# Operand sums of the Strassen pairs moved into a reordered output projection, with 2 plain pairs ahead instead of 3

## Chip, core, metric

The kernel runs on one core of one Trainium2 chip. The metric is device microseconds of one execution, median of three runs.

## What is computed

One residual block of a streaming encoder, on x of 512 tokens by 1024 channels in float32. The parts that matter here are its last lines; `merged` is the gated sum of two attention branches.

```python
x = x + merged @ w_out
h2 = rmsnorm(x, g_ffn)
ff = silu(h2 @ w_ffn_gate) * (h2 @ w_ffn_up)     # 1024 -> 2816
x = x + ff @ w_ffn_down                          # 2816 -> 1024
```

## The kernel before, in words

Channels lie on the 128 partitions, tokens on the free axis, so an activation is a list of tiles of 128 by 512. Each float32 operand is split into a high and a low fp32r part, and every product is three matmuls (`mm3`, L205 to L209: high by high, high by low, low by high). A weight block of 128 by 1024 is loaded into a ring of 5 raw buffers (`wraw`, N_RAW). ScalarE (ACT) casts the high part `wh`, VectorE (DVE) subtracts to get the low part `wl`, both in rings of 4 (`wspl`). `Stream` (L97 to L142) does this for a list of weights in order, four loads ahead. A raw buffer is free for its next load when the `wl` of its old content is done, and the load is issued by the SP queue, which also issues the loads and stores below.

The **output projection** (L905 to L922) has 8 blocks, one per 128 output channels. Block d is 24 matmuls of 512 columns into one of four PSUM banks (`full_ct(mg)`). A residual tile `xr` is loaded from `xT` (L907), DVE adds the PSUM bank to it (L909, "the residual add"), SP stores the sum to `x2_scratch` (L910), ACT and DVE split it, scaled by the norm's gain, into `h2h` and `h2l` (L914, L915), ACT squares it (L918), and POOL adds the squares up (L922). The loads, splits and adds are put in an order for each engine by a scheduler, from the program's order.

Then come 22 **pairs**: gate and up projection of 128 channels of ff each. `KINDS` (L32) says which are plain and which are Strassen. A plain pair is 48 matmuls of 512 columns. A Strassen pair (L798 to L894) is one step of Strassen's scheme on a 2 by 2 split of weights and tokens: 7 products of 12 matmuls of 256 columns. Its right operands are tiles of h2 and the sums `s13` and `s24` of tiles k and 4 + k, made by `operand_sums(k)` (L927 to L939) for k = 0 to 3. That function first scales the two `xr` tiles in place on ACT, after their store to `x2_scratch` has read them; then DVE takes sums, ACT casts high parts, and DVE subtracts low parts.

Before, pairs 0, 1 and 2 are plain and run in a loop of their own (L943 to L973) by the scheduler, with weights out of the `Stream`. In pair 0 one matmul, `pn` (L947), sums the squares over the partitions, and ACT and DVE make the norm factor `r2` from it. The four operand sums stand in pairs 1 and 2. From pair 3 on (L986 to L1015) PE, DVE and ACT keep the order in which the program is written, with loads (`load`, `load_t`) two and three pairs ahead. Pair 21 is plain. The down projection follows (L1019 to L1031).

Of the kernel before, what the change touches and what calls it, by code (L numbers as in the profile page):

```python
# [10 lines left out]
F32R = mybir.dt.float32r  # L11
AF = mybir.ActivationFunctionType
ALU = mybir.AluOpType
AX = mybir.AxisListType

P = 128
S = 512
D = 1024
KT = D // P
# [8 lines left out]
N_BLK, N_RAW, N_SPLIT = 66, 5, 4  # L28
DA_ROUNDS, DA_STAGGER, DA_LEAD = 31, 7, 6
SB_ROUNDS, SB_STAGGER = 36, 4  # L30
N_FIRST = 3
KINDS = "PPP" + "S" * 18 + "P"  # L32


def units(kind, a, b):
# [9 lines left out]
def block_kernel(  # L45
# [17 lines left out]
    nc = tc.nc  # L63
# [11 lines left out]
    def B(dt=F32, name="b"):  # L75
        uid[0] += 1
        return blk.tile([P, S], dt, tag="b", name=f"{name}{uid[0]}")

    def PS(name="ps"):
        uid[0] += 1  # L80
        if name in ("pt", "pc"):
            return psf.tile([P, S], F32, tag="pf", name=f"{name}{uid[0]}")
        return psp.tile([P, S], F32, tag="ps", name=f"{name}{uid[0]}")

    def f(ap):
        return ap.bitcast(F32)
# [10 lines left out]
    class Stream:  # L97
# [35 lines left out]
        def next(self):  # L133
            i = self.at
            self.at += 1
            if i >= self.own:
                for j in range(i, i + self.SPLIT):
                    self.split(j)
            for j in range(i, i + self.AHEAD + 1):
                if j not in self.hl:  # L140
                    self.load(j)
            return self.hl.pop(i)  # L142

    srcs = [w_tc[i, c] for i in range(2) for c in range(4)]
# [9 lines left out]
        else:  # L154
            srcs.append(w_br[i, 1])
    srcs += [w_br[d, 0] for d in range(8)]
    srcs += [w_out[d] for d in range(8)]
    for n in range(N_FIRST):
        srcs += [w_fg[n], w_fu[n]]
    wd = Stream(  # L160
# [6 lines left out]
    for kt in range(KT):  # L167
# [4 lines left out]
        sl = slice((kt % 2) * S, (kt % 2 + 1) * S)  # L172
        nc.sync.dma_start(out=ws.raw[kt // 2][0][:, sl], in_=srcs[kt // 2][:, sl])
    g_mix, g_ffn, b_gate, g_sub = colt[:, 0:8], colt[:, 8:16], colt[:, 16:32], colt[:, 32:33]
# [7 lines left out]
    epst = const.tile([P, 1], F32, name="epst")  # L182
# [3 lines left out]
    ones = const.tile([P, S], F32, name="ones")  # L186
# [18 lines left out]
    def mm3(ps, w, a, first, last):  # L205
        (wh, wl), (ah, al) = w, a
        nc.tensor.matmul(out=ps, lhsT=wh, rhs=ah, start=first, stop=False)  # L207
        nc.tensor.matmul(out=ps, lhsT=wh, rhs=al, start=False, stop=False)  # L208
        nc.tensor.matmul(out=ps, lhsT=wl, rhs=ah, start=False, stop=last)  # L209
# [31 lines left out]
    def proj_ct(ps, acts, first=True, last=True, stream=None):  # L241
        wh, wl = (stream or ws).next()
        n = len(acts)
        for kt in range(n):
            sl = slice(kt * P, (kt + 1) * P)
            mm3(ps, (wh[:, sl], wl[:, sl]), acts[kt], first and kt == 0, last and kt == n - 1)
            if kt % 4 == 3 or kt == n - 1:
                yield

    def drain(gen):  # L250
        for _ in gen:
            pass
# [6 lines left out]
    def full_ct(acts, **kw):  # L259
        ps = kw.pop("ps", None) or PS("pc")  # L260
        drain(proj_ct(ps, acts, **kw))
        return ps
# [3 lines left out]
    acc = B(name="acc")  # L266
    nc.scalar.activation(out=acc, in_=xts[0], func=AF.Square)
    for kt in range(1, KT):
        sq = B(name="xsq")
# [435 lines left out]
    mg = []  # L705
    for d in range(8):
        ps = full_ct(o_a)
        nc.vector.tensor_tensor(out=gA[d], in0=gA[d], in1=ps, op=ALU.mult)
        nc.vector.tensor_tensor(out=gA[d], in0=gA[d], in1=mB[d], op=ALU.add)
        h, l = B(F32R, "mh"), B(F32R, "ml")  # L710
# [7 lines left out]
    def tt(o, a, b, op=ALU.add):  # L718
        nc.vector.tensor_tensor(out=o, in0=a, in1=b, op=op)  # L719
# [22 lines left out]
    class Plain(Pair):  # L742
# [23 lines left out]
        def prep_c(self):  # L766
            pass

        def matmuls(self, ps, hl, kts):
            for kt in kts:  # L770
                sl = slice(kt * P, (kt + 1) * P)
                mm3(ps, (hl[0][:, sl], hl[1][:, sl]), h2[kt], kt == 0, kt == KT - 1)

        def steps(self):
            self.pg, self.pu = PS("pc"), PS("pq")
# [119 lines left out]

    pairs = [(Strassen if k == "S" else Plain)(n) for n, k in enumerate(KINDS)] + [None] * 4

    def call(n, what):
        if n < NF:
            getattr(pairs[n], what)()  # L900

    x2d = nc.dram_tensor("x2_scratch", (KT, P, S), F32, kind="Internal").ap()
    x2, h2 = [], []
    acc = None
    for d in range(8):  # L905
        xr = B(name="xr")
        nc.sync.dma_start(out=xr, in_=xT[:, d])  # L907
        ps = full_ct(mg)
        nc.vector.tensor_tensor(out=xr, in0=ps, in1=xr, op=ALU.add)  # L909
        nc.sync.dma_start(out=x2d[d], in_=xr)  # L910
        x2.append(xr)
        h, l = B(F32R, "h2h"), B(F32R, "h2l")
        gc = g_ffn[:, d : d + 1]
        nc.scalar.activation(out=h, in_=xr, func=AF.Copy, scale=gc)  # L914
        nc.vector.scalar_tensor_tensor(out=l, in0=xr, scalar=gc, in1=f(h), op0=ALU.mult, op1=ALU.subtract)  # L915
        h2.append((h, l))
        sq = B(name="x2s")
        nc.scalar.activation(out=sq, in_=xr, func=AF.Square)  # L918
        if acc is None:
            acc = sq  # L920
        else:
            nc.gpsimd.tensor_tensor(out=acc, in0=acc, in1=sq, op=ALU.add)  # L922

    s13 = [(B(F32R, "s13h"), B(F32R, "s13l")) for _ in range(KT // 2)]
    s24 = [(B(F32R, "s24h"), B(F32R, "s24l")) for _ in range(KT // 2)]

    def operand_sums(k):  # L927
        u, v = x2[k], x2[4 + k]
        for d, y in ((k, u), (4 + k, v)):
            nc.scalar.activation(out=y, in_=y, func=AF.Copy, scale=g_ffn[:, d : d + 1])  # L930
        sa, sb = B(name="sa"), B(name="sb")
        tt(sa[:, lo_t], v[:, hi_t], u[:, hi_t], ALU.subtract)
        tt(sa[:, hi_t], u[:, lo_t], u[:, hi_t], ALU.subtract)
        split(*s13[k], sa)
        for o, a, b in ((lo_t, sa[:, lo_t], u[:, lo_t]), (hi_t, v[:, lo_t], sb[:, lo_t])):
            nc.vector.scalar_tensor_tensor(
                out=sb[:, o], in0=a, scalar=-1.0, in1=b, op0=ALU.mult, op1=ALU.subtract
            )
        split(*s24[k], sb)  # L939

    r2 = B(name="r2")
    ff = []
    for n in range(N_FIRST):  # L943
        pg = full_ct(h2)
        if n == 0:
            pn = PS("pn2")
            nc.tensor.matmul(out=pn, lhsT=ones[:, 0:P], rhs=acc, start=True, stop=True)  # L947
            nc.scalar.activation(out=r2, in_=pn, func=AF.Sqrt, scale=1.0 / D, bias=epst)
            nc.vector.reciprocal(out=r2, in_=r2)
            call(N_FIRST, "load_t")  # L950
        if n == 1:
            call(N_FIRST, "load")
            call(N_FIRST + 1, "load_t")
            operand_sums(0)
        if n == 2:
            call(N_FIRST + 1, "load")
            call(N_FIRST, "cast_a")
            call(N_FIRST, "low_a")
            call(N_FIRST + 2, "load_t")
            operand_sums(2)  # L960
        t1 = B(name="t1")
        nc.vector.tensor_tensor(out=t1, in0=pg, in1=r2, op=ALU.mult)
        nc.scalar.activation(out=t1, in_=t1, func=AF.Silu)
        pu = full_ct(h2)
        if n == 1:
            operand_sums(1)
        if n == 2:
            operand_sums(3)
            for what in ("sums", "prep_b", "prep_c"):
                call(N_FIRST, what)  # L970
            call(N_FIRST + 1, "cast_a")
        nc.vector.tensor_tensor(out=t1, in0=pu, in1=t1, op=ALU.mult)
        ff.append(t1)  # L973

    fs = []

    def split_ff():
# [5 lines left out]
    ET = mybir.EngineType  # L983
    last = max(n for n in range(NF) if KINDS[n] == "S")
    prev = None
    with tc.manual_schedule(engines={ET.PE, ET.DVE, ET.Activation}):  # L986
        for n in range(N_FIRST, NF):
            call(n + 2, "load")
            call(n + 3, "load_t")
            if prev:  # L990
                prev.silu()
                prev.tail()
            steps = pairs[n].steps()
            next(steps)
            call(n + 1, "low_a")
            if prev:
                prev.mul()
            call(n + 1, "sums")
            next(steps)
            call(n + 1, "prep_b")  # L1000
            next(steps)
            call(n + 1, "prep_c")
            if n > last:
                for j in range(3):
                    wd.load((n - last - 1) * 2 + j)
                for _ in range(6):
                    split_ff()
            if n == NF - 1:
                wd.split(0)
            next(steps)  # L1010
            call(n + 2, "cast_a")
            prev = pairs[n]
        prev.silu()
        prev.tail()
        prev.mul()  # L1015
# [3 lines left out]
    for d in range(8):  # L1019
        xr = B(name="xo")  # L1020
        nc.sync.dma_start(out=xr, in_=x2d[d])
        ps = full_ct(fs[0:8], last=False, stream=wd)
# [3 lines left out]
        for i in range(parts):  # L1026
            sl = slice(i * S // parts, (i + 1) * S // parts)
# [66 lines left out]
```

## Time and profile before

| What | Value |
|---|---|
| median of 3 runs | 731.52 us (731.46 to 731.79) |
| profiled execution | 732.07 us, span of its instructions 730.4 us |
| PE (TensorE matmul) busy | 722.8 us, 99% |
| DVE busy | 522.1 us, 71% |
| ACT busy | 367.1 us, 50% |
| DMA | 91.69 MB, mean 126 GB/s |

The profiled execution is 0.55 us above the median, and 1.7 us of it lie around the span. Busy time of PE is modelled from overlapping matmuls, so a PE shown as busy can still be late; starts of matmuls tell more. PE, PEld, DVE, ACT and POOL are compute engines, SP is the queue that issues most transfers.

### The profile page before, as it was taken

Reading aid. Unit: us, or ns where it says so; the run is one execution under the profiler, and the core shown is the slowest. Engines: PE = TensorE matmul, PEld = TensorE weight load, DVE = VectorE, ACT = ScalarE, POOL = GpSimd, SP = SyncE. Lnnn points to the kernel's source line nnn. Section 1 sums busy time; section 2 is a strip of 40 time slices with the busy share of each in tenths; the row PEclk is TensorE's granted clock in tenths of the full one; section 3 lists DMA queues with packets and bytes.
Section 4 is the critical chain, followed back from the end, with each engine's and each line's share of the span. In section 5 each row is a group of like instructions: output and inputs, shape, how many; then the busy total and the mean of one; then the engine's idle time right before and its main releaser. Section 6 shows DMA issues by size and latency. Waiting matters only on the chain.

```text
span 730.4 us, 10841 instructions
## 1 busy us (share of the span) xinstructions
PE 722.8 (99%) x4054; PEld 629.5 (86%) x4054; DVE 522.1 (71%) x871; ACT 367.1 (50%) x594; POOL 91.8 (13%) x135
## 2 busy tenths in 40 slices
PE   9999999999999999999999999999999999999997
PEld 6888788888888878888887899999999998888886
DVE  5865888777578887988447899999999978323330
ACT  5732666878566665644555544445445456221210
POOL 0267000000033222300220011111110000000000
PEclk9999999999999999999999999999999999999999
DMA  8953131122222121245653187776676124444300
GB/s 307 314 148 111 58 116 58 63 83 73 72 87 88 46 70 31 71 138 164 217 174 129 62 212 200 181 187 169 178 199 174 52 60 152 155 131 118 114 29 30
DMA packets 40068, 91.69 MB, mean 126 GB/s; under 512 B 4432, under 2 KB 5072, under 8 KB 40016
## 3 DMA queue, kind: packets, MB, share of 16 engines
q1 hardware_dynamic: 34832, 81.41, 34.4%
q0 software_dynamic: 4896, 9.44, 7.6%
q8 instruction: 32, 0.52, 0.3%
q10 hardware_dynamic: 288, 0.15, 0.1%
q14 instruction: 20, 0.16, 0.1%
HBM read 84.69 MB, written 4.19 MB: 122 GB/s over the span
## 4 chain that ended last, share of the span: by engine, by line
PE 89%; DMA 4%; DVE 3%; issue 2%; ACT 1%; POOL 1%; SPq 0%; DVEq 0%; POOLq 0%; ACTq 0%
PE pc L207 19%; PE pc L208 19%; PE pc L209 19%; PE pt L223 9%; PE pq L208 4%; PE pq L207 4%; PE pq L209 4%; PE pk L223 3%; DMA xr<-xT_dram 3%; PE sc L412 1%; PE sc L413 1%; DVE wl L90 1%; DVE xr L909 1%; PE ta L418 1%; PE tb L418 1%
## 5 line engine op out<-in xcount | busy, mean ns | idle before, releaser
L90 DVE TENSOR_TENSOR wl<-raw,wh 128x1024 fp32r<-128x1024 f32 (+2 forms) x98 | 106.1, 1084 | 85.4 <-ACT wh L89 76.9
L89 ACT CAST wh<-raw 128x1024 fp32r<-128x1024 f32 (+2 forms) x98 | 90.8, 930 | 151.7 <-PE pc L208 98.2
L207 PE MATMUL pc<-hh,wh 128*128 128x512 f32 x192 | 76.2, 397 | 0.0
L209 PE MATMUL pc<-hh,wl 128*128 128x512 f32 x192 | 75.3, 392 | 0.0
L208 PE MATMUL pc<-hl,wh 128*128 128x512 f32 x192 | 75.0, 391 | 0.0
L207 PE MATMUL pc<-fh,wh 128*128 128x512 f32 x176 | 68.5, 389 | 0.0
L208 PE MATMUL pc<-fl,wh 128*128 128x512 f32 x176 | 68.5, 389 | 0.0
L209 PE MATMUL pc<-fh,wl 128*128 128x512 f32 x176 | 68.5, 389 | 0.0
L806 POOL DMA_DIRECT2D t<-w_fg_dram x18 | 21.7, 1208 | 184.4 <-DVE tb L719 63.3
L209 PEld LDWEIGHTS pc<-hh,wl 128*128 128x128 f32 x192 | 36.0, 188 | 7.7
L208 PEld LDWEIGHTS pc<-hl,wh 128*128 128x128 f32 x192 | 36.1, 188 | 6.6
L207 PEld LDWEIGHTS pc<-hh,wh 128*128 128x128 f32 x192 | 36.1, 188 | 6.6
L207 PE MATMUL pc<-s13h,wht 128*128 128x256 f32 x144 | 40.8, 283 | 0.0
L208 PE MATMUL pc<-s13l,wht 128*128 128x256 f32 x144 | 40.8, 283 | 0.0
L209 PE MATMUL pc<-s13h,wlt 128*128 128x256 f32 x144 | 40.8, 283 | 0.0
L207 PEld LDWEIGHTS pc<-fh,wh 128*128 128x128 f32 x176 | 33.0, 188 | 6.9
L209 PEld LDWEIGHTS pc<-fh,wl 128*128 128x128 f32 x176 | 33.0, 188 | 6.9
L208 PEld LDWEIGHTS pc<-fl,wh 128*128 128x128 f32 x176 | 33.0, 188 | 6.7
L548 POOL TENSOR_SCALAR_AFFINE_SELECT om<-om 128x128 f32<-128x128 f32 x32 | 12.7, 398 | 202.8 <-ACT om L545 196.8
L737 ACT CAST whx<-rx 128x1024 fp32r<-128x1024 f32 x18 | 19.0, 1054 | 28.2 <-PE pq L208 17.5
L737 ACT CAST whv<-tb 128x512 fp32r<-128x512 f32 x36 | 20.7, 619 | 23.0 <-issue 15.7
L223 PE MATMUL pt<-wh,hh 128*128 128x512 f32 x96 | 30.5, 403 | 0.1
(287 smaller groups left out, 2048.4 us busy)
## 6 DMA issues: line engine op xcount, KB each, us to landing
t<-w_fg_dram POOLq DMA_DIRECT2D x18, 512.0 KB, 8.0
raw<-w_gate_dram SPq DMA_DIRECT2D x16, 512.0 KB, 3.2
raw<-w_dn_dram SPq DMA_DIRECT2D x16, 512.0 KB, 3.6
raw<-w_tc_dram SPq DMA_DIRECT2D x12, 512.0 KB, 5.0
t<-w_fu_dram SPq DMA_DIRECT2D x18, 256.0 KB, 5.9
t<-w_fg_dram SPq DMA_DIRECT2D x18, 256.0 KB, 6.7
rx<-w_fu_dram SPq DMA_DIRECT2D x18, 256.0 KB, 3.5
rx<-w_fg_dram SPq DMA_DIRECT2D x18, 256.0 KB, 4.4
```

Source lines behind the costliest of these rows:

```text
L89: a = nc.scalar.copy(out=h, in_=src)
L90: b = nc.vector.tensor_tensor(out=l, in0=src, in1=f(h), op=ALU.subtract)
L207: nc.tensor.matmul(out=ps, lhsT=wh, rhs=ah, start=first, stop=False)
L208: nc.tensor.matmul(out=ps, lhsT=wh, rhs=al, start=False, stop=False)
L209: nc.tensor.matmul(out=ps, lhsT=wl, rhs=ah, start=False, stop=last)
L223: nc.tensor.matmul(out=pss[tb], lhsT=hx[:, tb * P : (tb + 1) * P], rhs=wx[:, wsl], start=(k == 0 and i == 0), stop=(k == KT - 1 and i == 2),)
L412: nc.tensor.matmul(out=ps[:, o : o + w], lhsT=q[:, tb * P : w], rhs=kh[:, :w], start=True, stop=False)
L413: nc.tensor.matmul(out=ps[:, o : o + w], lhsT=q[:, tb * P : w], rhs=kl[:, :w], start=False, stop=True)
L418: nc.tensor.transpose(out=ps[:, off + (tb - sb) * P : off + (tb - sb + 1) * P], in_=tiles[tb][:, sb * P : (sb + 1) * P], identity=ident,)
L548: nc.gpsimd.affine_select(out=t[:, o + w - P : o + w], in_=t[:, o + w - P : o + w], pattern=[[-1, P]], compare_op=ALU.is_gt, fill=fill, ba ...
L737: nc.scalar.copy(out=hl[0], in_=src)
L806: nc.gpsimd.dma_start(out=self.t13.rearrange("p (a b) -> p a b", b=S), in_=w_fg[n, :, lo_w].unsqueeze(1).broadcast_to([P, 2, S]), accum_op ...
```

## The change

The output projection runs in the order 0, 4, 1, 5, 2, 6, 3, 7 (`D_ORDER`), so that tiles k and 4 + k are done one after the other. `operand_sums` 0, 1 and 2 are called inside it, after its blocks at place 2, 4 and 6; `operand_sums(3)` is called in the first steps of pair 0. `N_FIRST` is 0: the loop for the first pairs is gone, all 22 pairs run in the hand order, and pairs 0 and 1 are plain with their own loads (`load`, L743 to L749 before) in place of the `Stream`. Pair 2 is now a Strassen pair, 19 in all. Plain pairs take their tiles of h2 in `D_ORDER`. Line numbers of the changed kernel are 1 to 2 higher up to the pairs' classes.

```diff
-N_FIRST = 3
-KINDS = "PPP" + "S" * 18 + "P"
+N_FIRST = 0
+KINDS = "PP" + "S" * 19 + "P"
+D_ORDER = (0, 4, 1, 5, 2, 6, 3, 7)
...
-    srcs += [w_out[d] for d in range(8)]
+    srcs += [w_out[d] for d in D_ORDER]
...
-    for d in range(8):
+    for j, d in enumerate(D_ORDER):
         xr = B(name="xr")
         nc.sync.dma_start(out=xr, in_=xT[:, d])
         ps = full_ct(mg)
         nc.vector.tensor_tensor(out=xr, in0=ps, in1=xr, op=ALU.add)
         nc.sync.dma_start(out=x2d[d], in_=xr)
...
+        if j == 4:
+            call(0, "load")
+            call(2, "load_t")
+        if j == 6:
+            call(0, "cast_a")
+            call(0, "low_a")
+            call(1, "load")
+        if j == 7:
+            call(0, "prep_b")
+        if j in (2, 4, 6):
+            operand_sums(j // 2 - 1)
...
-    for n in range(N_FIRST):
-        pg = full_ct(h2)
-        if n == 0:
-            pn = PS("pn2")
...
             steps = pairs[n].steps()
             next(steps)
+            if n == 0:
+                operand_sums(3)
+                call(1, "cast_a")
             call(n + 1, "low_a")
...
             call(n + 1, "prep_b")
+            if n == 0:
+                pn = PS("pn2")
+                nc.tensor.matmul(out=pn, lhsT=ones[:, 0:P], rhs=acc, start=True, stop=True)
```

What this does to the order of the instructions, at three places. In the names, `xr512`, `xr517`, `xr522` are the residual tiles of the blocks at place 0, 1, 2 in both programs. Those at place 3 to 7 are `xr527`, `532`, `537`, `542`, `547` before and `xr533`, `538`, `549`, `554`, `565` now. `raw64` to `raw69` are the weights of pairs 0 to 2 before, `rg` and `ru` those of a plain pair now, and `rx` is a Strassen pair's two half blocks.

The SP queue from the load ahead of the third residual add's store on, before:

```order
L110 DMA raw67_3777<-w_fu_dram 128x1024
L910 DMA x2_scratch<-xr522_3560 128x512
L907 DMA xr527_3602<-xT_dram 128x512
L110 DMA raw68_3834<-w_fg_dram 128x1024
L910 DMA x2_scratch<-xr527_3602 128x512
L907 DMA xr532_3644<-xT_dram 128x512
L110 DMA raw69_3876<-w_fu_dram 128x1024
L910 DMA x2_scratch<-xr532_3644 128x512
L907 DMA xr537_3686<-xT_dram 128x512
```

And now, from that store on:

```order
L930 DMA x2_scratch<-xr522_3560 128x512
L816 DMA rx2_3871<-w_fu_dram 128x512
L817 DMA rx2_3871<-w_fg_dram 128x512
L927 DMA xr533_3618<-xT_dram 128x512
L816 DMA rx3_3963<-w_fu_dram 128x512
L930 DMA x2_scratch<-xr533_3618 128x512
L927 DMA xr538_3660<-xT_dram 128x512
L817 DMA rx3_3963<-w_fg_dram 128x512
L930 DMA x2_scratch<-xr538_3660 128x512
L816 DMA rx4_4048<-w_fu_dram 128x512
L817 DMA rx4_4048<-w_fg_dram 128x512
L927 DMA xr549_3724<-xT_dram 128x512
```

Before, each residual load (L907) stands right behind the store of the block before it. Now the two loads of `rx2` stand ahead of the one for place 3, and the two of `rx4` ahead of the one for place 5.

DVE after the third residual add (`xr522`), where the last `w_out` block, `raw63`, is split; before:

```order
L90 TENSOR_TENSOR wl63_3732<-raw63_3609,wh63_3731 128x1024
L909 TENSOR_TENSOR xr527_3602<-pc528_3604,xr527_3602 128x512
L915 SCALAR_TENSOR_TENSOR h2l530_3638<-xr527_3602,colt_79,h2h529_3637 128x512
L90 TENSOR_TENSOR wl64_3774<-raw64_3651,wh64_3773 128x1024
L909 TENSOR_TENSOR xr532_3644<-pc533_3646,xr532_3644 128x512
```

And now:

```order
L720 TENSOR_TENSOR sa531_3608<-xr517_3518,xr512_3477 128x256
L720 TENSOR_TENSOR sa531_3608<-xr512_3477 128x256
L91 TENSOR_TENSOR s13l528_3605<-sa531_3608,s13h527_3604 128x512
L919 SCALAR_TENSOR_TENSOR sb532_3609<-sa531_3608,xr512_3477 128x256
L91 TENSOR_TENSOR wl63_3768<-raw63_3625,wh63_3767 128x1024
L919 SCALAR_TENSOR_TENSOR sb532_3609<-xr517_3518,sb532_3609 128x256
L91 TENSOR_TENSOR s24l530_3607<-sb532_3609,s24h529_3606 128x512
L720 TENSOR_TENSOR wlg0_3805<-rg0_3700,whg0_3804 128x1024
L929 TENSOR_TENSOR xr533_3618<-pc534_3620,xr533_3618 128x512
```

Most of the first operand sum now stands ahead of the split of `raw63`, and `wlg0` ahead of the next residual add.

DVE at the last two residual adds, before:

```order
L909 TENSOR_TENSOR xr542_3728<-pc543_3730,xr542_3728 128x512
L90 TENSOR_TENSOR wl66_3873<-raw66_3735,wh66_3872 128x1024
L915 SCALAR_TENSOR_TENSOR h2l545_3764<-xr542_3728,colt_79,h2h544_3763 128x512
L909 TENSOR_TENSOR xr547_3770<-pc548_3772,xr547_3770 128x512
L90 TENSOR_TENSOR wl67_3905<-raw67_3777,wh67_3904 128x1024
```

And now:

```order
L929 TENSOR_TENSOR xr554_3764<-pc555_3766,xr554_3764 128x512
L935 SCALAR_TENSOR_TENSOR h2l557_3798<-xr554_3764,colt_79,h2h556_3797 128x512
L720 TENSOR_TENSOR sa563_3818<-xr549_3724,xr538_3660 128x256
L720 TENSOR_TENSOR sa563_3818<-xr538_3660 128x256
L91 TENSOR_TENSOR s13l560_3815<-sa563_3818,s13h559_3814 128x512
L919 SCALAR_TENSOR_TENSOR sb564_3819<-sa563_3818,xr538_3660 128x256
L919 SCALAR_TENSOR_TENSOR sb564_3819<-xr549_3724,sb564_3819 128x256
L91 TENSOR_TENSOR s24l562_3817<-sb564_3819,s24h561_3816 128x512
L929 TENSOR_TENSOR xr565_3828<-pc566_3830,xr565_3828 128x512
```

The third operand sum now stands whole between the seventh and the last residual add.

## Rows read from the trace of the kernel before

**Rows 1.** Stages: length, busy time and count by engine, PEclk granted clock, DMA share, GB/s

```profile
336.00:379.46 43.46, 43.46 (x193) 35.73 (x192) 23.69 (x29) 22.66 (x30) 6.87 (x6) 1.00 0.57 182
379.46:413.69 34.23, 34.01 (x148) 27.52 (x147) 24.58 (x38) 17.60 (x23) 2.66 (x2) 1.00 0.29 92
413.69:423.77 10.08, 10.08 (x86) 10.07 (x84) 9.98 (x17) 6.56 (x10) 1.20 (x1) 1.00 0.63 195
...
730.00:731.00 1.00, 0.00 (x0) 0.00 (x0) 0.00 (x0) 0.00 (x0) 0.00 (x0) 0.77 0.00 0
```

**Rows 2.** Timeline of PE: start, length, line, tiles, [idle before <- releaser]

```profile
384.45 0.39 PE L207 MATMUL pc<-h2h,wh 128*128 128x512 f32 x1
...
385.52 1.12 PE L947 MATMUL pn<-x2s,ones 128*128 128x512 f32 x2 [0.22 <-POOL x2s L922]
...
391.94 0.39 PE L207 MATMUL pc<-h2h,wh 128*128 128x512 f32 x1
...
413.69 0.28 PE L207 MATMUL pc<-h2h,whx 128*128 128x256 f32 x1
...
423.77 0.28 PE L207 MATMUL pc<-h2h,whx 128*128 128x256 f32 x1
```

**Rows 3.** Chain that ended last: start, length, what (a DMA from issue to landing)

```profile
355.83 5.47 DMA xr<-xT_dram
...
372.59 4.29 DMA xr<-xT_dram
...
378.06 3.68 DMA xr<-xT_dram
...
725.65 0.24 PE pc L209
```

**Rows 4.** Timeline of the SP queue in the output projection

```profile
362.04 0.33 SPq L910 DMA_DIRECT2D x_scratch<-xr  x1
362.46 0.38 SPq L907 DMA_DIRECT2D xr<-xT_dram  x1
```

**Rows 5.** DMA issues, 300 to 420 us: count, KB each, median us to landing

```profile
b<-w_fu_dram SPq DMA_DIRECT2D x3, 256.0 KB, 4.5
```

**Rows 6.** Timeline of DVE at residual adds, a split and an h2l

```profile
354.70 0.68 DVE L909 TENSOR_TENSOR xr<-pc,xr 128x512 f32<-128x512 f32 x1
356.18 0.75 DVE L915 SCALAR_TENSOR_TENSOR h2l<-xr,colt,h2h 128x512 fp32r<-128x512 f32 x1 [0.80 <-ACT h2h L914]
359.00 1.22 DVE L90 TENSOR_TENSOR wl<-raw,wh 128x1024 fp32r<-128x1024 f32 x1 [2.07 <-ACT wh L89]
...
381.83 0.69 DVE L909 TENSOR_TENSOR xr<-pc,xr 128x512 f32<-128x512 f32 x1 [2.38 <-DMA xr<-xT_dram]
```

**Rows 7.** Timeline of ACT: a cast of weights, and the last h2h

```profile
357.91 1.06 ACT L89 CAST wh<-raw 128x1024 fp32r<-128x1024 f32 x1 [1.24 <-PE pc L208]
...
382.56 0.73 ACT L914 ACTIVATE h2h<-xr,colt 128x512 fp32r<-128x512 f32 x1 [1.00 <-DVE xr L909]
```

**Rows 8.** Timeline of DVE in one operand sum of pair 2

```profile
409.43 0.42 DVE L719 TENSOR_TENSOR sa<-xr,xr 128x256 f32<-128x256 f32 x1
...
410.87 0.69 DVE L90 TENSOR_TENSOR s13l<-sa,s13h 128x512 fp32r<-128x512 f32 x1 [0.69 <-ACT s13h L89]
...
413.05 0.69 DVE L90 TENSOR_TENSOR s24l<-sb,s24h 128x512 fp32r<-128x512 f32 x1 [0.69 <-ACT s24h L89]
413.66 0.68 DVE L719 TENSOR_TENSOR tb<-t,rx 128x512 f32<-128x512 f32 x1
```

**Rows 9.** Timeline of PE at the start of the kernel

```profile
1.55 3.78 PE L190 MATMUL warm<-ones 128*128 128x512 f32 x4 [1.55 <-DVE ones L187]
5.47 1.84 PE L223 MATMUL pt<-wh,hh 128*128 128x512 f32 x4
7.15 1.09 PE L223 MATMUL pt<-wh,hl 128*128 128x512 f32 x4
```

**Rows 10.** Transfers of x_scratch, issue to landing

```profile
DMA to landing us min/median/max: 2.0/3.7/4.1
```

More of the change, by code (lines that the diff above doesn't have):

```diff
@@ L767, in prep_c, with matmuls @@
             pass
-        def matmuls(self, ps, hl, kts):
-            for kt in kts:
+        def matmuls(self, ps, hl, ks):
+            for k in ks:
+                kt = D_ORDER[k]
                 sl = slice(kt * P, (kt + 1) * P)
-                mm3(ps, (hl[0][:, sl], hl[1][:, sl]), h2[kt], kt == 0, kt == KT - 1)
+                mm3(ps, (hl[0][:, sl], hl[1][:, sl]), h2[kt], k == 0, k == KT - 1)
         def steps(self):
@@ L902, in block_kernel @@
     x2d = nc.dram_tensor("x2_scratch", (KT, P, S), F32, kind="Internal").ap()
-    x2, h2 = [], []
-    acc = None
-    for d in range(8):
[L906 to L925, printed above, removed]
+    x2, h2 = [None] * KT, [None] * KT
+    s13, s24 = [], []
     def operand_sums(k):
@@ L930, in operand_sums @@
             nc.scalar.activation(out=y, in_=y, func=AF.Copy, scale=g_ffn[:, d : d + 1])
+        s13.append((B(F32R, "s13h"), B(F32R, "s13l")))
+        s24.append((B(F32R, "s24h"), B(F32R, "s24l")))
         sa, sb = B(name="sa"), B(name="sb")
@@ L939, in operand_sums @@
         split(*s24[k], sb)
+    acc = None
+    for j, d in enumerate(D_ORDER):
+        xr = B(name="xr")
+        nc.sync.dma_start(out=xr, in_=xT[:, d])
+        ps = full_ct(mg)
+        nc.vector.tensor_tensor(out=xr, in0=ps, in1=xr, op=ALU.add)
+        nc.sync.dma_start(out=x2d[d], in_=xr)
+        x2[d] = xr
+        h, l = B(F32R, "h2h"), B(F32R, "h2l")
+        gc = g_ffn[:, d : d + 1]
+        nc.scalar.activation(out=h, in_=xr, func=AF.Copy, scale=gc)
+        nc.vector.scalar_tensor_tensor(out=l, in0=xr, scalar=gc, in1=f(h), op0=ALU.mult, op1=ALU.subtract)
+        h2[d] = (h, l)
+        sq = B(name="x2s")
+        nc.scalar.activation(out=sq, in_=xr, func=AF.Square)
+        if acc is None:
+            acc = sq
+        else:
+            nc.gpsimd.tensor_tensor(out=acc, in0=acc, in1=sq, op=ALU.add)
+        if j == 4:
[9 more added lines that the diff above has]
+            operand_sums(j // 2 - 1)
     r2 = B(name="r2")
     ff = []
-    for n in range(N_FIRST):
-        pg = full_ct(h2)
-        if n == 0:
-            pn = PS("pn2")
[L947 to L973, printed above, removed]
     fs = []
@@ L1000, in block_kernel @@
             call(n + 1, "prep_b")
+            if n == 0:
+                pn = PS("pn2")
+                nc.tensor.matmul(out=pn, lhsT=ones[:, 0:P], rhs=acc, start=True, stop=True)
+                nc.scalar.activation(out=r2, in_=pn, func=AF.Sqrt, scale=1.0 / D, bias=epst)
+                nc.vector.reciprocal(out=r2, in_=r2)
             next(steps)
```

## Prediction

> **What bounds the kernel now.** I read the stages first, then PE's starts, then the chain of waits, then the queues that the chain names. The stages [rows 1] show TensorE busy for all of the output projection (43.46 of 43.46 us) and for all but 0.22 us of the three plain pairs behind it. What ends last here is PE, and any time that PE stands still is paid in full, since nothing later has slack: from the first Strassen pair on PE is full too. The starts of matmuls [rows 2] give the prices: plain pairs 1 and 2 take 391.94 to 413.69, 10.87 us each, a Strassen pair 413.69 to 423.77, 10.08 us.
>
> Next comes how near the cover is to running out. The chain [rows 3] does not run through PE in the output projection but through residual loads: each waits in the SP queue behind the store of the block before it, which waits for that block's residual add. The third add starts at 354.70 [rows 6] and the next load is issued at 355.83 [rows 3]; SP issues a load right behind the store [rows 4]. One turn of this ring (add, store issue, load, add) takes about as long as a block, 5.4 us. The last add starts at 381.83 [rows 6], its `h2h` ends at 383.29 [rows 7], and pair 0 needs it at 384.45 [rows 2]: 1.2 us to spare. Behind it comes `pn`, which starts 3.69 us after the last add and is the one thing that waits, for 0.22 us of idle time, on POOL [rows 2]. So whatever delays the last add moves `pn` and all behind it, one for one.
>
> **The change, part by part.**
>
> *Pair 2 becomes a Strassen pair.* 10.87 less 10.08 is a gain of 0.8 us on PE. Its work on DVE and ACT has the cover of 10.08 us of PE as in the pair shown, where DVE is busy for 9.98 us [rows 1]; without that cover it would cost its excess over 10.08. Cost taken: none. Own loads for pairs 0 and 1 in place of the stream move the same bytes: none. `pn` stays behind the first 24 matmuls of pair 0.
>
> *The residual loads.* This is where I expect the loss. The raw ring has 5 buffers, so `rx2` takes that of `raw63`, `rx3` that of `rg0`, `rx4` that of `ru0`, and each load waits in SP until DVE has done the low part of the old content. SP issues in order; a store or residual load behind such a wait is held. Before, `raw63`'s successor stood behind a residual load, now `rx2` stands ahead of one. Step by step, with places 0 to 7 for the blocks; up to the add of place 2 both programs are alike.
>
> 1. Add 2 at 354.70, its `h2l` at 356.18 [rows 6]. DVE is free for the next operation of 512 columns after 0.61 us (413.05 to 413.66, [rows 8]), so the first `sa` starts at 356.8. The high part of `s13` is done 1.44 us after `sa` starts [rows 8], at 358.2. Only then ACT casts `raw63`, 1.06 us [rows 7], to 359.3, and DVE takes 1.22 us [rows 6], to 360.5. Two loads of `rx2` at 0.42 us each [rows 4], and the residual load of place 3 leaves at 361.4. Before it left at 355.83: 5.5 us, one block, is lost.
> 2. It is the third of three loads of 256 KB in a row; the third of such a group took 4.5 us at the median [rows 5]. Add 3 at 365.9. (`wlg0` stands ahead of it on DVE: its buffer is free with the end of block 4, 363.3, then 1.06 and 1.22 make 365.6, so it hides.)
> 3. From add to next load 1.13 us, as from 354.70 to 355.83: 367.0. One `rx3` load ahead and one behind, as with the load that took 4.29 us [rows 3]. Add 4 at 371.3.
> 4. DVE then does `wlu0`, 371.9 to 373.1, for which `rx4` waits. Its two issues take 0.84 us, the load of place 5 leaves at 374.0, and with 4.5 us add 5 is at 378.5. (The second operand sum ends before that.)
> 5. 1.13 us and 3.68 us, the time of a load with nothing ahead of it [rows 3]: add 6 at 383.3.
> 6. Add 7's load lands by 388.1, but DVE has the third operand sum in front: 1.48 us from add to `h2l`, 0.61, then 4.23 us for the sum (409.43 to 413.66, [rows 8]). Add 7 at 389.6.
>
> That is 7.8 us after 381.83, and `pn` slips as much. Ends: with every load at 3.68 us, `wlg0` sets add 3 at 365.6, the second sum sets add 5 at 377.0, and add 7 is at 388.1, a slip of 6.3. With every load at the longest, 5.47 us [rows 3], add 7 is at 394.5, a slip of 12.7. I take the rows of like neighbours, 7.8.
>
> These loads are where a rule of the Trainium skill differs. The page "DMA: Bandwidth & Descriptors", section "Anatomy of one DMA — SWDGE (gpsimd) path", fits a transfer as 2.0 us plus its bytes at 436 GB/s, 2.6 us for 256 KB (an estimate by that page, whose fit is for POOL's path, not SP's). By it add 7 would be at 386.1 and the time some 735; the rows above, of SP's own loads, have 3.68 us and more, so the sum goes by them.
>
> *TensorE's clock.* In pair 0 the second last step was due at 383.77 (three matmuls before 384.45) and now finds `h2h` at 384.8 (add 6 plus 1.46, as from 381.83 to 383.29): 1.0 us idle. After three matmuls, stretched by their `h2l`, the last step waits from about 386 to 391.1, 5.1 us; with all loads at 3.68 us it is still 5.0. What such a stop does to the clock shows only at the end of the trace: the last matmul ends at 725.9 [rows 3], and 0.77 granted over 730 to 731 [rows 1] means that it fell from 2.4 to 1.2 GHz about 730.5, 4.6 us later. At the lower level four matmuls took 1.68 us, 5.47 to 7.15, against 0.91 at the pace of a plain pair (10.87 us for 48); that pace held from the first matmul, 1.55, to about 7.15, 5.6 us [rows 9]. If it falls in the wait of 5.1 us and stays low for 5.6 us from 391.1, then PE has `pn` to wait for until 393.3 anyway, and the 3.4 us to 396.7 run at half pace: 1.7 us lost. Ends: nothing if the clock holds, 2.8 us if all 5.6 us count. The nearest row is the fall after 4.6 us, so I take 1.7.
>
> The Trainium skill's page "TensorE: Matmul & The Clock Gate", section "HAM oscillation — how this bites in real kernels", speaks against the change in the same way: waits for DMA between short runs of matmuls bring the clock down, and each such wait is paid again at the lower pace. By that rule the time is the forecast below, without it the second case.
>
> **Sum.** Slip 7.8, clock 1.7, less 0.8: 8.7 us more. On the profiled execution of 732.07 us that is 740.8; on the median, 0.55 us below it, 740.2. I say 740.0.
>
> **The rivals.**
>
> - *The clock holds.* The stop is only 0.5 us longer than the one that ended in a fall, and one fall is little to go by. Then 731.5 plus 7.8 less 0.8: 738.5.
> - *Not slower: the residual loads still run ahead of their need.* The mechanism is the SP ring above; it decides by the last add. Up to 383.0 or so `h2h` is there in time and PE sees nothing. For that the loads of `rx2` and `rx4` must not hold the queue, for example because `raw63` is split by the time SP gets there. Then pair 2's 0.8 us stay, and up to 0.4 us of `pn`'s wait goes: 730.3. Against it: the order puts both pairs of loads ahead, and the third sum alone takes 4.23 us ahead of the last add. For it: only that PE had 1.2 us to spare.
> - *A shorter slip.* If transfers are quicker than any row here, DVE's work (wlg0, two sums) still holds the last add at about 386: 735 with the clock held.
> - *Pair 1's weights.* `whg1` and `wlg1` stand behind the last sum, which waits for the last store, 2.0 to 4.1 us [rows 10]. Pair 1 is due at 391.94 plus 7.8; at 4.1 us its low part would be up to 1 us late. At 2.0 us it is in time. This only shifts the slower cases up by 1 us at most.
>
> **How the numbers follow.** Forecast (slip and fall) 0.50; slip with the clock held 0.33; a shorter slip 0.08; not slower 0.09. A change of 0.2%, 1.46 us, is about what can be told from none; faster by more than that needs over 1.5 us and I find 1.2, so faster gets 0.02 and same 0.07 out of the not slower case, slower 0.91. The range starts at 735, the shorter slip, which leaves out the 0.09, and ends at 743.0: the forecast with some 3 us of longer loads or a later pair 1, leaving out 0.08 of the slow end (743.4 with every load at its longest, more with a fall).
>
> **What would show it.** In the changed profile the SP queue should show the residual load of place 3 leaving near 361.4 behind two `rx` loads, and the last residual add near 390. PE should be idle about 1 us and about 5 us, released by the `h2h` cast, inside the first 24 matmuls of pair 0, and `pn` should start near 393. The granted clock should be under 1.00 in the stage after 391; if it is 1.00, the second case holds. Strassen pairs should still take 10.08 us, and PE should have no other gaps. I am wrong if PE passes from the output projection into pair 0 without idle time, or if a stall arises in pair 1 or 2 instead.

## The result, and the profile after

The changed kernel takes **741.52 us** (median of 4 runs, 741.15 to 743.0) where the kernel before, on the same chip, takes 731.65 us (4 runs, 731.46 to 732.24): a ratio of 1.0134, 95% interval 1.0123 to 1.0146, 9.87 us slower. The profiled execution took 741.75 us, 9.68 us above that of before (732.07). Its page:

```profile
span 740.1 us, 10935 instructions
...
PE 724.9 (98%) x4090; PEld 631.2 (85%) x4090; DVE 531.1 (72%) x882; ACT 368.7 (50%) x598; POOL 92.7 (13%) x136
```

The span is 9.7 us longer and PE is busy for only 2.1 us more (722.8 before). So most of the loss must be idle time of PE. The table of PE's waits says where:

```profile
PE pc L208 <- ACT h2h L934: 7.0, 2, 5.9
```

One line waits twice for the `h2h` cast, once for 5.9 us. The timeline of PE places it inside pair 0 (start, length, line, tiles, idle time before and its releaser):

```profile
379.87 0.39 PE L208 MATMUL pc<-h2h,whg 128*128 128x512 f32 x1
...
385.18 0.51 PE L208 MATMUL pc<-h2h,whg 128*128 128x512 f32 x1 [1.06 <-ACT h2h L934]
...
386.30 0.40 PE L210 MATMUL pc<-h2h,wlg 128*128 128x512 f32 x1
392.63 0.80 PE L208 MATMUL pc<-h2h,whg 128*128 128x512 f32 x1 [5.93 <-ACT h2h L934]
...
394.57 2.08 PE L989 MATMUL pn<-x2s,ones 128*128 128x512 f32 x2
...
402.64 0.39 PE L208 MATMUL pc<-h2h,whg 128*128 128x512 f32 x1
```

`pn` starts at 394.57 against 385.52 before [rows 2]. Before, pair 0 starts here:

```profile
379.69 0.39 PE L207 MATMUL pc<-h2h,wh 128*128 128x512 f32 x1
```

The whole trace thus runs 0.18 us late ahead of pair 0 (379.87, not 379.69), so the slip is 8.87 us. From `pn` to the start of pair 1 (402.64) it takes 8.07 us against 6.42 before (385.52 to 391.94, [rows 2]): 1.65 us more. Less 0.80 for pair 2 that is 9.72 us. From the start of pair 0 to the last matmul of the kernel it is 9.73 us more (379.87 to 735.40 against 379.69 to 725.49), so these three terms are all of it.

Why `h2h` is late stands in the SP queue:

```profile
361.84 0.33 SPq L816 DMA_DIRECT2D rx<-w_fu_dram  x1
362.22 0.43 SPq L817 DMA_DIRECT2D rx<-w_fg_dram  x1
362.74 0.38 SPq L927 DMA_DIRECT2D xr<-xT_dram  x1
...
373.37 0.33 SPq L816 DMA_DIRECT2D rx<-w_fu_dram  x1
374.05 0.33 SPq L817 DMA_DIRECT2D rx<-w_fg_dram  x1
374.44 0.41 SPq L927 DMA_DIRECT2D xr<-xT_dram  x1
...
384.77 0.42 SPq L927 DMA_DIRECT2D xr<-xT_dram  x1
```

The residual load of place 3 leaves at 362.74, behind the two loads of `rx2`; before it left at 355.83 [rows 3]. That of place 5 leaves behind `rx4`, that of place 7 at 384.77. And in DVE, from the first sum to the last residual add (L929):

```profile
357.02 1.53 DVE L720 TENSOR_TENSOR sa<-xr,xr 128x256 f32<-128x256 f32 x1
...
360.59 1.23 DVE L91 TENSOR_TENSOR wl<-raw,wh 128x1024 fp32r<-128x1024 f32 x1
...
366.29 0.69 DVE L929 TENSOR_TENSOR xr<-pc,xr 128x512 f32<-128x512 f32 x1 [0.46 <-DMA xr<-xT_dram]
...
371.52 0.69 DVE L929 TENSOR_TENSOR xr<-pc,xr 128x512 f32<-128x512 f32 x1 [2.99 <-DMA xr<-xT_dram]
...
379.23 0.68 DVE L929 TENSOR_TENSOR xr<-pc,xr 128x512 f32<-128x512 f32 x1
...
383.68 0.69 DVE L929 TENSOR_TENSOR xr<-pc,xr 128x512 f32<-128x512 f32 x1 [2.21 <-DMA xr<-xT_dram]
...
385.82 1.52 DVE L720 TENSOR_TENSOR sa<-xr,xr 128x256 f32<-128x256 f32 x1
...
390.53 0.69 DVE L91 TENSOR_TENSOR s24l<-sb,s24h 128x512 fp32r<-128x512 f32 x1 [0.68 <-ACT s24h L90]
391.13 0.68 DVE L929 TENSOR_TENSOR xr<-pc,xr 128x512 f32<-128x512 f32 x1
```

Three of these adds wait for a load; those of place 5 and 7 (379.23, 391.13) start without idle time, right behind the end of a sum. The first `sa` of a sum takes 1.5 us here and 0.42 in pair 2 of the kernel before [rows 8].

The chain of waits that ends last runs through both, one after the other: the first sum, three residual loads, and the two other sums (start, length, what).

```profile
357.10 1.80 DVE sa L720 x2
...
362.74 3.53 DMA xr<-xT_dram
...
367.43 4.06 DMA xr<-xT_dram
...
374.00 1.77 DVE sa L720 x2
...
380.36 3.22 DMA xr<-xT_dram
...
385.90 1.78 DVE sa L720 x2
```

So the wait in the SP queue is itself behind a sum: the loads of `rx2` leave when `wl` of `raw63` ends (360.59 plus 1.23), and that split stands behind most of the first sum.

The clock, by stages (length, busy time and count of PE, PEld, DVE, ACT, POOL, then the granted clock, DMA share, GB/s):

```profile
383.00:386.00 3.00, 1.66 (x7) 0.80 (x6) 1.54 (x3) 1.24 (x2) 0.21 (x1) 1.00 0.26 96
386.00:387.50 1.50, 0.69 (x2) 0.26 (x2) 1.50 (x2) 0.00 (x0) 1.06 (x1) 1.00 0.57 165
387.50:388.00 0.50, 0.00 (x0) 0.00 (x0) 0.17 (x1) 0.29 (x1) 0.00 (x0) 0.72 0.02 8
388.00:390.00 2.00, 0.00 (x0) 0.00 (x0) 1.45 (x3) 1.07 (x3) 0.00 (x0) 0.50 0.00 0
...
397.50:398.00 0.50, 0.50 (x2) 0.41 (x2) 0.28 (x1) 0.19 (x1) 0.00 (x0) 0.54 0.00 0
```

0.72 granted over 387.5 to 388 means that it fell from 2.4 to 1.2 GHz at 387.72, and 0.54 that it rose again at 397.96.

### The profile page after: what moved, and what is told of

It reads as the page before. It is cut to its first block, busy times and chain, and to the rows that moved or that the text cites. A ratio compares the mean times of both kernels' runs of the same rounds, so it can differ in the third digit from the quotient of the medians.

```text
span 740.1 us, 10935 instructions
## 1 busy us (share of the span) xinstructions
PE 724.9 (98%) x4090; PEld 631.2 (85%) x4090; DVE 531.1 (72%) x882; ACT 368.7 (50%) x598; POOL 92.7 (13%) x136
## 4 chain that ended last, share of the span: by engine, by line
PE 88%; DVE 4%; DMA 3%; issue 2%; ACT 1%; POOL 0%; SPq 0%; DVEq 0%; POOLq 0%; ACTq 0%
PE pc L208 18%; PE pc L209 18%; PE pc L210 18%; PE pt L224 9%; PE pq L208 4%; PE pq L210 4%; PE pq L209 4%; PE pk L224 3%; DMA xr<-xT_dram 2%; PE sc L413 1%; PE sc L414 1%; DVE sa L720 1%; PE ta L419 1%; DVE wl L91 1%; PE tb L419 1%
## 5 line engine op out<-in xcount | busy, mean ns | idle before, releaser
L90 ACT CAST wh<-raw 128x1024 fp32r<-128x1024 f32 (+2 forms) x92 | 84.4, 921 | 143.9 <-PE pc L209 87.5
L91 DVE TENSOR_TENSOR wl<-raw,wh 128x1024 fp32r<-128x1024 f32 (+2 forms) x92 | 98.2, 1069 | 78.3 <-ACT wh L90 74.1
L208 PE MATMUL pc<-s13h,wht 128*128 128x256 f32 x152 | 43.0, 283 | 0.0
L209 PE MATMUL pc<-s13l,wht 128*128 128x256 f32 x152 | 43.0, 283 | 0.0
L210 PE MATMUL pc<-s13h,wlt 128*128 128x256 f32 x152 | 43.0, 283 | 0.0
L720 DVE TENSOR_TENSOR wlv<-tb,whv 128x512 fp32r<-128x512 f32 x38 | 24.5, 687 | 10.7 <-ACT whv L738 10.7
```

What stands on the lines that cost most here:

```text
L90: a = nc.scalar.copy(out=h, in_=src)
L91: b = nc.vector.tensor_tensor(out=l, in0=src, in1=f(h), op=ALU.subtract)
```

## The experiments

Each is the changed kernel with the edit shown, unless said otherwise, timed beside the kernel before on the same chip; the medians of before there were 732.3 us (experiments 1 to 4), 731.92 (5 to 8) and 731.63 (9 and 10). Line numbers move by up to 6 with an edit.

| Experiment | us, median | ratio to before | 95% interval |
|---|---|---|---|
| the change | 741.52 | 1.0134 | 1.0123 to 1.0146 |
| 1 residual loads early | 730.72 | 0.9981 | 0.9972 to 0.9990 |
| 2 sums later | 743.56 | 1.0153 | 1.0139 to 1.0167 |
| 3 needless matmuls | 739.71 | 1.0102 | 1.0087 to 1.0118 |
| 4 squares on DVE | 739.08 | 1.0098 | 1.0083 to 1.0113 |
| 5 SP's order by hand | 741.53 | 1.0124 | 1.0104 to 1.0143 |
| 6 third sum later | 739.93 | 1.0106 | 1.0088 to 1.0124 |
| 7 one plain pair, loads early | 733.43 | 1.0018 | 1.0007 to 1.0029 |
| 8 kernel before, loads early | 731.82 | 0.9994 | 0.9985 to 1.0004 |
| 9 as 5, last load moved up | 737.52 | 1.0087 | 1.0070 to 1.0104 |
| 10 as 9, third sum later | 736.21 | 1.0057 | 1.0042 to 1.0072 |

**1. Do the residual loads carry the loss?** All eight are issued ahead of the projection.

```diff
+    xrs = []
+    for d in D_ORDER:
+        xr = B(name="xr")
+        nc.sync.dma_start(out=xr, in_=xT[:, d])
+        xrs.append(xr)
     for j, d in enumerate(D_ORDER):
-        xr = B(name="xr")
-        nc.sync.dma_start(out=xr, in_=xT[:, d])
+        xr = xrs[j]
```

> The changed kernel with one edit: the eight residual loads are issued ahead of the output projection, so none stands behind a store or behind the loads of rx2 and rx4. Theory (the residual loads held in the SP queue make the loss): the residual adds follow their blocks, the last one is before 383 us, PE has no idle time over 0.5 us in pair 0, the clock stays at 1.00, about 730.3 us. Rival 1 (the operand sums on DVE hold the adds, the loads only add to it): the last add still comes some 2 to 3 us late, about 733 us. Rival 2 (the loss is in the hand order or the 19th Strassen pair): near 741 us.

730.72 us: the whole loss is gone, and both kernels are beaten, the one before by 0.2%. The last residual add, in DVE's timeline:

```profile
380.50 0.68 DVE L933 TENSOR_TENSOR xr<-pc,xr 128x512 f32<-128x512 f32 x1
```

and `pn`, in PE's, without a wait:

```profile
385.08 1.02 PE L993 MATMUL pn<-x2s,ones 128*128 128x512 f32 x2
```

The adds now follow their blocks. This does not yet part the SP queue from the sums: with the loads landed the scheduler also puts an add into the middle of the first sum (358.78, between the two halves of `sb`), so both causes went at once. The sums themselves are still there, and hold the last add back by no more than 0.7 us (its block ends at 379.8), for which PE does not wait: the third sum starts at 376.54 here, behind a seventh add at 374.39, and not at 385.82.

**2. Are the sums in the projection the cause?** They are taken out of it; two run in pair 0 and two in pair 1.

```diff
-        if j in (2, 4, 6):
-            operand_sums(j // 2 - 1)
...
-                operand_sums(3)
...
+            if n < 2:
+                operand_sums(2 * n)
...
+            if n < 2:
+                operand_sums(2 * n + 1)
```

> The changed kernel with the four operand sums taken out of the output projection and put into pairs 0 and 1, where the kernel before has them (pairs 1 and 2 there); order of the blocks, 2 plain pairs, 19 Strassen pairs and the hand order stay. Theory: rx2's loads stand behind the residual load again, the last add is near 382 us, no idle time of PE over 0.5 us, 730.5 to 731 us. Rival (the hand order from the first pair on, or pairs 0 and 1 with their own loads, cost by themselves): more than 733 us.

A miss: 743.56 us. In the projection things went as expected (last add at 381.03, no wait of PE in pair 0, `pn` at 385.15), so the hand order and the own loads of pairs 0 and 1 cost nothing there. But the sums then come too late for pair 2:

```profile
408.95 0.58 PE L208 MATMUL pc<-s24h,whx 128*128 128x256 f32 x1 [4.26 <-ACT s24h L90]
414.84 0.58 PE L208 MATMUL pc<-s24h,whx 128*128 128x256 f32 x1 [4.38 <-ACT s24h L90]
```

In this order two plain pairs are too little cover for four sums, the 3.35 us of the reciprocal and the preparation of the next weights on DVE. DVE also stands idle for 3.41 us ahead of the reciprocal (until 386.93), behind which the first sum was put, but that is less than the 8.6 us of these two waits. So with this order of the work inside the two pairs the sums have to begin ahead of pair 0; that no other order would do is not shown.

**3. What does the clock cost?** Needless matmuls keep PE at work in the two waits of pair 0; their bank is never read.

```diff
                 kt = D_ORDER[k]
+                if self.n == 0 and ps is self.pg and k >= 6:
+                    idle = PS("idle")
+                    for _ in range(5 if k == 6 else 26):
+                        nc.tensor.matmul(out=idle, lhsT=hl[0][:, 0:P], rhs=h2[0][0], start=True, stop=True)
```

> The changed kernel with 5 and 26 needless matmuls of 512 columns (into a bank that nobody reads) on PE in the two places of pair 0 where it waits, so that it works through about 1.1 and 5.9 us. Theory (the fall of the clock is a cost of its own, 1.8 us after pn): the clock is 1.00 throughout, pn starts where it did, pair 1 starts 1.8 us earlier, 739.7 us. Rival (the clock costs nothing, because what follows waits for something else): the same 741.5 us. Rival 2 (the needless matmuls end later than the wait): above 741.5.

```profile
394.20 1.13 PE L993 MATMUL pn<-x2s,ones 128*128 128x512 f32 x2 [0.42 <-POOL x2s L946]
...
400.63 0.39 PE L208 MATMUL pc<-h2h,whg 128*128 128x512 f32 x1
```

739.71 us, as expected, with a granted clock of 1.00 throughout pair 0. `pn` follows the last add by 3.44 us in both (391.13 to 394.57, here 390.76 to 394.20, where it waits for POOL), so the low clock costs nothing ahead of `pn`. From `pn` to pair 1 it takes 6.43 us here (394.20 to 400.63) and 8.07 in the changed kernel: the clock costs **1.64 us**. The other 0.37 us of the spans' difference (738.0 to 740.1) is an earlier last add.

**4. Why does `sa` take 1.5 us?** In the changed kernel POOL adds squares in the very same stretches:

```profile
356.98 1.29 POOL L942 TENSOR_TENSOR x2s<-x2s,x2s 128x512 f32<-128x512 f32 x1 [3.63 <-ACT x2s L938]
...
385.79 1.27 POOL L942 TENSOR_TENSOR x2s<-x2s,x2s 128x512 f32<-128x512 f32 x1 [3.16 <-ACT x2s L938]
```

POOL ends at 358.27 and at 387.06; `sa`, begun 0.03 to 0.04 us after POOL began, ends 0.28 us behind POOL both times (357.02 plus 1.53, 385.82 plus 1.52). The fourth sum, in pair 0, starts when POOL is done (394.79 against 394.51), and its `sa` takes 0.43 us. So the squares are added on DVE instead:

```diff
-            nc.gpsimd.tensor_tensor(out=acc, in0=acc, in1=sq, op=ALU.add)
+            nc.vector.tensor_tensor(out=acc, in0=acc, in1=sq, op=ALU.add)
```

> The changed kernel with the squares added up on DVE in place of POOL. Theory (the first operation of each operand sum takes 1.5 in place of 0.42 us because POOL adds squares at the same time): the first sa takes 0.42 us in all four sums, each sum is 1.1 us shorter, against 0.6 us per add of squares on DVE; about 740 to 741.5 us. Rival (it is slow for another reason, such as the tiles it reads): it still takes 1.5 us, and the time is 742 us or more.

```profile
385.02 0.42 DVE L720 TENSOR_TENSOR sa<-xr,xr 128x256 f32<-128x256 f32 x1
```

739.08 us. All sums now have `sa` at 0.42 or 0.43 us, though DVE has more to do: it was POOL's addition that held `sa` up. The last add comes 1.89 us earlier (389.24) and `pn` 2.03 (392.54). The ratio falls by 0.0036, some 2.6 us, a little more than expected: the clock is low again only until 394.40, and `pn` to pair 1 takes 7.25 us in place of 8.07. The Trainium skill's page "SBUF — State Buffer", section "Who interferes with whom", states that a VectorE instruction with two inputs in SBUF contends with a GpSimd instruction that reads SBUF, that the shared ports are an exclusive lock, and that the order of issue decides which of the two is blocked. The trace agrees in the main: `sa` came second and ended 0.28 us behind POOL, where 0.42 would be its whole length.

**5. SP's order alone, first try.** The residual loads, their stores and the pairs' loads are held to the program's order.

```diff
-            nc.sync.dma_start(out=self.g, in_=w_fg[self.n])
+            pinned([nc.sync.dma_start(out=self.g, in_=w_fg[self.n])])
...
-        nc.sync.dma_start(out=xr, in_=xT[:, d])
+        pinned([nc.sync.dma_start(out=xr, in_=xT[:, d])])
```

> The changed kernel with SP's order set by hand, so that the pairs' loads that wait for a ring buffer stand behind the residual loads of places 3 and 5; the sums stay where the change puts them. Theory (the slip comes from SP's order, and only the third sum, 5.3 us, then stands ahead of the last residual add): the add of place 6 comes near 377 us, that of place 7 near 384.4, TensorE waits some 2 us in pair 0 in place of 7.2, and the time is near 733.3 if the clock holds, near 735 if it falls. Rival (the sums on VectorE make the whole slip, whatever SP's order): 740 or more, with a wait near 5.9 us as in the changed kernel.

Theory and rival were both wrong in part: 741.53 us. The add of place 3 comes at 362.04 in place of 366.29, those of place 5 and 6 2.9 us earlier (376.33, 380.78). But two loads of pair 1 and two of `rx` now stand ahead of the residual load of place 7, and the chain of waits shows what became of it:

```profile
377.46 3.22 DMA xr<-xT_dram
...
384.07 6.40 DMA xr<-xT_dram
```

With the DMA engines busy for 0.86 to 1.02 of the time from 386 to 392 us it takes 6.40 us, twice the usual, and the last add is at 390.56. The add of place 6, expected near 377, came at 380.78: turns from one add to the next with a sum took 8.3 and 9.9 us, those without 4.4. The edit also does more than reorder `rx2` and `rx4`: pair 0's own loads, at 339.25 and 344.78 in the changed kernel, now leave at 367.58 and 368.05, and the splits of these weights stand in the turn of 9.9 us, ahead of the add of place 5 (`wlu` at 375.19). So neither 5 nor 9 is a clean test of the queue alone.

**6. Is the third sum in the way?** It is moved behind the last residual add.

```diff
-        if j in (2, 4, 6):
-            operand_sums(j // 2 - 1)
+        if j in (2, 4, 7):
+            operand_sums(j // 3)
```

> The changed kernel with the third operand sum moved behind the last residual add, SP's order as in the changed kernel. Theory (the last add waits for that sum, its load lands 2.6 us before the add starts): the last add comes near 388.5 us, 2.6 us earlier, and the time is 738.9 us if the clock falls as it does there, near 737.1 if it holds; the weights of pair 1 stand behind two sums and may cost up to 1 us. Rival (the sum is not in the way, the load alone sets the last add): 741.5.

739.93 us, 0.0028 lower in the ratio, some 2 us, though the two intervals touch. The wait in pair 0 shrinks and a new one opens at pair 1:

```profile
389.28 0.62 PE L208 MATMUL pc<-h2h,whg 128*128 128x512 f32 x1 [2.85 <-ACT h2h L934]
...
399.89 0.50 PE L208 MATMUL pc<-h2h,whg 128*128 128x512 f32 x1 [1.23 <-ACT whg L738]
```

The last add is at 387.78, 3.35 us earlier: the sum was in the way. Of that 1.76 us go back at pair 1, whose `whg` and `wlg` stand behind two sums (1.23, and 0.53 for `wlg`). Up to 1 us had been allowed for this, on top of the 738.9 written.

**7. Would one plain pair do?** Experiment 1 with pair 1 a Strassen pair, too.

```diff
-KINDS = "PP" + "S" * 19 + "P"
+KINDS = "P" + "S" * 20 + "P"
...
+            call(1, "load_t")
             call(2, "load_t")
```

> The first experiment's kernel (all residual loads ahead of the projection) with one plain pair and 20 Strassen pairs. Theory (a Strassen pair is worth 0.8 us when nothing waits): 0.8 below that kernel, some 729.9 us. Rival (the fourth sum or the weights of pair 1 come too late once that pair is a Strassen pair): as the first experiment, 730.7, or above it, with a wait of TensorE at the start of pair 1.

The rival was right on the time: 733.43 us, 2.7 above experiment 1. PE waits in pair 1, though not at its start (391.69) but in its fourth product, for DVE, which has been busy throughout the stretch that PE stands still:

```profile
398.39 0.38 PE L208 MATMUL pc<-s13h,wht 128*128 128x256 f32 x1 [2.22 <-DVE t L720]
```

```profile
396.00:398.00 2.00, 0.17 (x2) 0.00 (x0) 2.00 (x4) 0.00 (x0) 0.00 (x0) 1.00 0.40 145
```

What PE waits for is `t` (397.65 to 398.33), which reads the bank of pair 0 and stands behind the reciprocal (393.25, 3.35 us). Fourth sum, reciprocal and a Strassen pair's preparations don't fit beside one plain pair. In the profiled executions this is the whole difference: pair 1 takes 12.54 us (391.69 to 404.23) against 10.88 in experiment 1 (391.42 to 402.30), 1.66 more, and so does the stretch from the start of pair 0 to the last matmul (346.21 against 344.55 us). The rest of the 2.7 us between the medians is a difference between executions: five of the ten took 732.7 to 733.0 us, the other five 733.9 to 734.6 at mean granted clocks of 0.996 to 0.998. No trace shows where those five lost it.

**8. Does the kernel before gain from early loads?** The same edit as in experiment 1, to the kernel before.

> The kernel before with the residual loads issued ahead of the projection. Theory (there they cost it nothing but the 0.4 us that the norm's matmul waits): 0.4 us below the kernel before, so within 0.2%, which leaves the Strassen pair as most of the gain of the first experiment. Rival (the early loads themselves make the gain): 1 us or more below the kernel before.

731.82 us, no change that can be measured in the time. Its PE waits nowhere in pair 0 (`pn` at 385.44). So early loads alone are not the gain of experiment 1. The intervals of 1 and 8 touch, so the times don't settle the sizes, but the traces do, for one execution each: from the start of pair 0 to the last matmul PE takes 345.80 us before (379.69 to 725.49), 345.35 here (379.99 to 725.34) and 344.55 in experiment 1 (379.63 to 724.18). That is 0.45 us for the early loads and 0.80 for the Strassen pair.

**9. SP's order alone, mended.** As 5, with the residual load of place 7 issued right behind that of place 6.

```diff
+        if j < 7:
             xr = B(name="xr")
             pinned([nc.sync.dma_start(out=xr, in_=xT[:, d])])
+        else:
+            xr = xr7
+        if j == 6:
+            xr7 = B(name="xr")
+            pinned([nc.sync.dma_start(out=xr7, in_=xT[:, D_ORDER[7]])])
```

> The fifth experiment's kernel (SP's order set by hand), with the residual load of place 7 issued right behind that of place 6, so that no load of a pair stands ahead of it. The sums stay where the change puts them. Theory now (with SP's order mended, the three sums on VectorE are the next bound: a turn with a sum takes 8 to 10 us, one without 4.4 us): the add of place 6 stays near 380.8 us and that of place 7 comes when the third sum ends, near 388.4 us, 2.2 us earlier than in the fifth experiment, with VectorE not idle before it; the time is near 739.3 us. Rival (only transfers make the slip): the last add comes as the load allows, near 385 us, and the time is near 735.5 us.

737.52 us, between the two. The last two adds run back to back from 380.55, so the add itself did not wait for the sum as I had written:

```profile
380.55 1.33 DVE L935 TENSOR_TENSOR xr<-pc,xr 128x512 f32<-128x512 f32 x2 [2.42 <-DMA xr<-xT_dram]
```

But on ACT the casts of the third sum stand ahead of the last `h2h`:

```profile
386.78 0.62 ACT L90 CAST s24h<-sb 128x512 fp32r<-128x512 f32 x1 [0.93 <-DVE sb L919]
387.30 0.72 ACT L940 ACTIVATE h2h<-xr,colt 128x512 fp32r<-128x512 f32 x1
```

The tile is ready at about 381.9 and its cast starts at 387.30; PE waits 3.38 us. The sum is still what the end waits for, now on ACT. In experiment 1 the same casts also stand ahead of the last `h2h`, but there the third sum starts at 376.54, not at 382.70, and `h2h` at 381.22: the sum is in the way in 9 because the adds ahead of it are late.

**10. Both.** As 9, with the third sum behind the last add, as in 6.

> The same, with the third operand sum also moved behind the last residual add. Theory (loads in order and one sum fewer ahead): the last add comes near 383 us, TensorE waits under 1 us in pair 0 and the clock holds there; the weights of pair 1 then stand behind two sums, 12.1 us behind the last add as in the sixth experiment, near 395 us, where pair 1 is due near 392.6 us, so TensorE waits some 2.5 us there; the time is near 734 us. Rival (the sums are not a bound once SP's order is mended): the same time as the kernel with the third sum in place, within 1 us.

```profile
385.63 1.13 PE L995 MATMUL pn<-x2s,ones 128*128 128x512 f32 x2 [0.25 <-POOL x2s L948]
...
394.53 0.50 PE L208 MATMUL pc<-h2h,whg 128*128 128x512 f32 x1 [2.29 <-ACT whg L738]
395.79 0.52 PE L210 MATMUL pc<-h2h,wlg 128*128 128x512 f32 x1 [0.52 <-DVE wlg L720]
```

The waits in pair 0 are gone, `pn` is where it was before the change, and pair 1 starts at 394.53 with 2.81 us of waits, as expected. The time, 736.21 us, is 2 us above what I wrote: the clock fell just after these waits (0.53 granted over 396 to 398), which I had not counted. One of the four executions kept a mean granted clock of 0.999, where the other three had 0.997, and took 734.26 us, as written.

## Why the prediction came out as it did

The forecast was 740.0 us with a fall of the clock; 741.52 us and a fall are the result. The mechanism was right; the slip was 1.1 us larger than said, as two errors of size with opposite signs partly made up for each other.

- **The SP queue** (steps 1 to 4): right in order and place. The load of place 3 left at 362.74 where 361.4 was said; 1.1 of these 1.3 us are the long `sa` of the first sum, the price that also failed in step 6. Experiment 9 mends the order, with the side effects named at 5, and gains some 3.4 us (0.0047 of the ratio). The prediction said "This is where I expect the loss". The loss does hang on the late loads, since it is gone in experiment 1 with the sums still in the projection; but what holds the loads back is in good part the sums, which are on the same chain of waits.
- **Loads** of place 3, 4 and 6: sized at 4.5, 4.3 and 3.7 us by rows of like neighbours, they took 3.53, 4.06 and 3.22. That was too long by 0.2 to 1 us each.
- **The operand sum**, sized at 4.23 us by [rows 8], took 5.3 (385.82 to 391.13). This term failed, in step 6 and in step 1: it was taken from a stretch in which POOL was not at work on the squares. It hid in part behind the shorter loads, which is luck: less the 0.18 us of the later trace, the adds of place 3 to 6 came within 0.6 us of what was said, place 5's by another releaser (the second sum, not its load).
- **Add 7** came at 391.13 in place of 389.6, and `pn` slipped by 8.87 in place of 7.8.
- **The clock**: 1.7 us forecast, 1.65 measured, 1.64 by experiment 3. That it fell was right, but it fell 1.0 us into the wait, where the end of the trace before had shown 4.6 us behind the last matmul [rows 1, 3]; over 383 to 386 PE had been busy for only 1.66 of 3.00 us. What counts for the size is the stretch from `pn` to the rise, 3.4 us in the forecast and 3.39 in fact (394.57 to 397.96). That these agree is in part luck. The forecast's 5.6 us come from a stretch where the matmuls are slow but the trace gives a granted clock of 1.00 (1.5 to 9 us). And `pn` to pair 1 took 7.25, 7.31 and 8.31 us in experiments 4, 5 and 9, where the clock fell in the same wait: 0.8 to 1.9 us above the 6.42 of before. The Trainium skill's page "TensorE: Matmul & The Clock Gate", section "HAM oscillation — how this bites in real kernels", which the prediction drew on, was right in kind: the wait was paid for a second time, at the lower pace.
- **The Strassen pair**: 0.8 us forecast, and pair 2 takes 10.08 us (413.52 to 423.60) against the 10.87 of a plain pair [rows 2].
- **The rivals**: the clock didn't hold. "Not slower" is what experiment 1 made true, by the mechanism named there. "Pair 1's weights" did not bite in the change itself, but did in experiments 6 and 10, at 1.8 and 2.8 us.

What stays open: how the 9 us divide between queue and sums can't be given as two numbers, since each holds the other back; and why about half of the executions of experiment 7 took a further 1.5 us.

## What to carry to other kernels

When work moves between two loops, follow each load queue and each engine that must keep its order: a load that waits for a buffer holds every later load of its queue, and a sum placed ahead of a short step that others wait for (here the last tile's add or cast) can delay that step, here by 3.35 us of the sum's 5.3 (experiment 6), unless the work ahead of the sum is early enough (experiment 1). Issue small inputs whose buffers are free well ahead, before such a queue gets crowded; here that turned a loss of 1.3% into a gain of 0.2%. Take the price of an operation from a stretch in which the neighbouring engines do what they will do in the new place.

## What was not expected of the hardware

DVE's subtraction of two SBUF tiles of 128 by 256 took 1.51 to 1.53 us beside a POOL addition of 1.3 to 1.5 us, and 0.42 alone (experiment 4). The granted clock fell 1.0 us into a wait and stayed low for 10.24 us, until 3.4 us behind `pn`; in experiment 4 it was low for 6.8 us (387.57 to 394.40), and in experiment 10 it fell at 396.14, when PE was already at work again. A transfer of 256 KB took 3.22 us with the DMA engines busy for 0.32 to 0.52 of the time (377 to 381) and 6.40 us with 0.86 to 1.02 (both experiment 5).
